# Storing some products of a gated feed-forward block as two split parts and loading the parts in place

## The chip, the cores and the metric

The kernel runs on one core of one Trainium2 chip. The metric is the time of one execution on the device in microseconds (us), lower is better. The engines are PE (TensorE), DVE (VectorE), ACT (ScalarE), POOL (GpSimd) and SP (SyncE, which here only issues DMAs). Each engine takes its instructions strictly in the order of its own list; an instruction that waits holds everything behind it on that engine.

## The reference

One layer works on x of 1024 tokens by 1024 channels in float32. The two feed-forward blocks (D_FF = 2816) are what the change touches:

```python
def swiglu(x, wg, wu, wd):
    return (jax.nn.silu(x @ wg) * (x @ wu)) @ wd

def reference(x, ...):
    x = x + 0.5 * swiglu(rmsnorm(x, norm_ffn1[l]), ffn1_wg[l], ffn1_wu[l], ffn1_wd[l])
    h = rmsnorm(x, norm_mix[l])
    ...  # one projection, an mLSTM group and an RG-LRU group, one output projection
    x = x + 0.5 * swiglu(rmsnorm(x, norm_ffn2[l]), ffn2_wg[l], ffn2_wu[l], ffn2_wd[l])
    return rmsnorm(x, norm_final)
```

## The kernel before

Activations lie with channels on the 128 partitions and tokens along the free axis, in two halves of 512 tokens. Every matmul is made three times, (high, high), (high, low) and (low, high): `split` (L107) writes a tile's high part with a CAST on ACT (L108) and its low part, the tile minus the high part, with a subtraction on DVE (L109).

`ffn` runs twice. Its inner product u = silu(gate) x up has 22 rows f of 128 channels. Rows 0 to 3 are made by `plain` (24 matmuls for each half and weight). Rows 4 to 21 are made in *units*: `Pair.run` (L543) multiplies a 2x2 block product with seven block products instead of eight. A unit has seven *steps* of 12 matmuls, s0 to s6, which use the factors B11, T1, T2, B21, T3, B22, T4 of the right-hand side in this order. s0, s2, s4 and s6 add up in one PSUM bank (X), s1 and s5 in another (Y), s3 has its own (Z). After each step `out(i, ...)` takes the running sum: out0, out1 and out2 are copies on ACT (`kept`, L613), out3 to out5 are additions on DVE (L617). So s2 must wait for out0, s4 for out2, s5 for out1 and s6 for out4, because each adds on to a bank that has to be read first.

The last product of the block, with wd, uses rows 0 to 15 of u in eight more units (`down`), in two groups of four. Their seven factors are sums and differences of u that `Sink` makes on POOL (`first_sum` L482: T1; `sums` L490 to L495: T2, T3, T4) when a pair of rows (f even, f odd) is there, and stores to DRAM (`f_d`, 1 MB each, `store` L463). Class `Stored` loads them back: `fetch(i)` brings factor i in plain float32 into a staging tile while the unit before is running, `split(i)` makes the two parts (L109 into `bop`) once that unit has finished step i. In the down units each `out` is a scaled copy on ACT (L646) that POOL adds to x with an accumulating DMA (L647). Rows 16 to 21 of u are stored whole (`u_d`), loaded by `act` and split, and go into an ordinary product at the end of the block (L325).

Temporary 128x512 tiles come from one pool of three buffers (`t2`, L100); rows f even of the first 16 lie in two tiles of their own (`even`). Odd rows, T4 and now and then a square use `t2`. Before the first block, `norm.square` takes the squares of x for the norm on ACT and adds them up on POOL (L184), tile by tile behind the loads.

The order on each engine is made by a scheduler when the program is built, from the written order and from costs of its own; it isn't what the chip finds ready at run time.

Of the kernel before, what the change touches and what calls it, by code (L numbers as in the profile page):

```python
# [8 lines left out]
F32 = mybir.dt.float32  # L9
R32 = mybir.dt.float32r  # L10
# [23 lines left out]
def hymba_block_kernel(ctx: ExitStack, tc, xT, chv, qkv, kblk, wgate, bgate, up1, db1, dn1, up2, db2,  # L34
# [13 lines left out]
    r_d = [dram.tile([P, T], F32, name=f"r_d{i}") for i in range(NK)]  # L48
    u_d = [dram.tile([P, T], F32, name=f"u_d{i}") for i in range(NF - 16)]
    f_d = [{n: dram.tile([P, 4, 512], F32, name=f"f_d{i}{n}")  # L50
            for n in ("B11", "T1", "T2", "B21", "T3", "B22", "T4")} for i in range(2)]
# [155 lines left out]
    class Norm:  # L207
# [22 lines left out]

        def square(self, xs, m, h, wait, first=1):
            add_square(self.pool, self.acc[h], row(xs, m)[:, half_of(h)], m)
            if m == NK - 1:
                def stats():
                    rs = row_rstd(self.pool, self.pool, self.acc[h][0], "n")
                    defer(wait, lambda: self.spread(xs, h, rs))
                defer(first, stats)
# [100 lines left out]
    def row(xs, t):  # L338
        return xs[t // 4][:, t % 4]
# [66 lines left out]
    class Stored:  # L406

        def __init__(self, bx, late, src):  # L410
            self.bx, self.late, self.src, self.ops, self.raw = bx, late, src, {}, {}

        def fetch(self, i):
            if i >= len(FACTORS):
                return
            src = self.src[FACTORS[i]].rearrange("p a n -> p (a n)")
            if i % 2 == 0:
                r = wup.tile([P, 2, T], R32, tag="wu", name="stage", bufs=4).bitcast(F32)
                nc.sync.dma_start(out=r.rearrange("p a n -> p (a n)"), in_=src)
                self.raw[i] = [r[:, 0], r[:, 1]]  # L420
            else:
                self.raw[i] = [raw_tile(), self.late.tile([P, T], F32, tag="rb_late", name="stage",
                                                          bufs=1)]
                for c, r in enumerate(self.raw[i]):
                    nc.sync.dma_start(out=r, in_=src[:, c * T:(c + 1) * T])

        def split(self, i):
            t = self.ops[FACTORS[i]] = factor_tile(self.bx, FACTORS[i])
            for c, r in enumerate(self.raw.pop(i)):
                split(t[:, 0, 2 * c:2 * c + 2], t[:, 1, 2 * c:2 * c + 2],  # L430
                      r.rearrange("p (a n) -> p a n", a=2))
# [18 lines left out]
    class Sink:  # L450
# [6 lines left out]
        def tile(self, f):  # L457
            if f < BLOCKED and f % 2 == 0:
                return self.pool.tile([P, 512], F32, tag="acc", name="even", bufs=2)
            return self.tmp()  # L460

        def store(self, f, name, t):
            nc.sync.dma_start(out=f_d[f // 8][name][:, f % 8 // 2], in_=t)  # L463

        def done(self, f, h, t):
            if f >= BLOCKED:
                nc.sync.dma_start(out=u_d[f - BLOCKED][:, half_of(h)], in_=t)
                return
            r = self.rows.setdefault(f, {})
            r[h] = t  # L470
            if f % 2 == 0:
                if h == 0:
                    self.store(f, "B11", t)
                if len(r) == 2:
                    self.pending.append(lambda: self.first_sum(f))
                return
            self.store(f, ("B21", "B22")[h], t)
            if len(r) == 2:
                self.flush()
                self.sums(f)  # L480

        def first_sum(self, f):  # L482
            u = self.rows[f]
            nc.gpsimd.tensor_tensor(out=u[0], in0=u[1], in1=u[0], op=ALU.subtract)
            self.store(f, "T1", u[0])

        def sums(self, f):
# [7 lines left out]
            sub(out=t, in0=v[0], in1=u[0], op=ALU.subtract)  # L495
            self.store(f, "T4", t)

        def flush(self):
# [74 lines left out]
    def ffn(xs, norm, up, blocked, dn, source, after_row, load_next=lambda: None, last_pieces=halves,  # L573
# [3 lines left out]
        with tc.tile_pool(name="bx", bufs=3, reuse_waits="tile") as bx:  # L577
            with tc.tile_pool(name="up", bufs=1, reuse_waits="tile") as pool:
# [73 lines left out]
                for g in range(BLOCKED // 8):  # L652
                    factors = Stored(bx, norm.pool, f_d[g])
                    work += [(Pair(pool, blocked[g, 2 * j], blocked[g, 2 * j + 1]), factors, down(j))
                             for j in range(4)]

                p = work[0][0]
                late = [plain(0, 0), plain(0, 1), plain(1, 0)]
                for f in late:
                    f()  # L660
                late = [plain(1, 1)]
                late.append(plain(0, 2))
                for f in late:
# [23 lines left out]
                def act(n):  # L687
                    t = half_tile(("a", n // 2), bx, "bx", n % 2)
                    acts[n] = t
                    split(t[:, 0], t[:, 1], load(u_d[n]))  # L690

# [56 lines left out]
    for h in range(2):  # L748
        for m in range(NK):
            nc.sync.dma_start(out=row(xs, m)[:, half_of(h)], in_=xT[m, :, half_of(h)])  # L750
            norm.scale(xs, m, h)
            norm.square(xs, m, h, 2, (2, 3)[h])
            if (h, m) in ((0, 0), (0, 1), (0, 5), (0, 7)):
                first.append((weights if first else weights_by_half)(up1[len(first)]))
    norm_mix = Norm(nrm, "nm")

# [747 lines left out]
```

## Time and profile before

| | |
|---|---|
| three runs | 2144.03, 2145.83, 2145.97 us; median 2145.83 |
| profiled execution | 2142.77 us, span of the trace 2141.1 us |
| PE busy | 2074.8 us (97%), 9526 matmuls |
| DVE, ACT, POOL busy | 1215.5 (57%), 921.9 (43%), 861.2 us (40%) |
| HBM read, written | 168.89 MB, 65.55 MB |

The profile lists when each instruction ran and what ended the idle time before it. The first feed-forward block takes the first 630 us or so of the span plus an ordinary product to about 700 us, the second the last 690 us. PE is nearly always busy, so what counts is where PE sits idle, and for what. PEclk is the clock granted to PE as a share of 2.4 GHz.

### The profile page before, as it was taken

The page shows a single profiled execution, that of the slowest core. Times are in us where ns is not written, and L with a number is a line of the kernel's source. Part 1 is how long each engine was busy: PE and PEld are TensorE (multiplying, and loading weights), DVE is VectorE, ACT ScalarE, POOL GpSimd, SP SyncE. Part 2 cuts the span into 40 slices and gives each one's busy share as a digit, 9 for nine tenths or more (in the row PEclk, how much of TensorE's full clock was granted, in tenths as well). Part 3 has the DMA queues.
Part 4 walks back from the last instruction along what each step waited for, and adds up shares of the span by engine and source line. Part 5 has one row for each costly group of instructions (what it writes and reads, how often), then busy time and mean ns, then how long its engine had stood idle before and what let it go on. Part 6 is the DMA issues. An engine that isn't in the chain of part 4 may idle for free.

```text
span 2141.1 us, 25174 instructions
## 1 busy us (share of the span) xinstructions
PE 2074.8 (97%) x9526; PEld 1708.2 (80%) x9526; DVE 1215.5 (57%) x1618; ACT 921.9 (43%) x1337; POOL 861.2 (40%) x614
## 2 busy tenths in 40 slices
PE   8999999999999999999999999999999999999998
PEld 6878888878778788878878888777888888877877
DVE  7954444473434455665538998878753444474334
ACT  5333333354542355555546554233333333365443
POOL 4465455445634212232311122433555555354623
PEclk9999999999999999999999999999999999999999
DMA  4143232278891311132246332121243323388852
GB/s 169 64 172 123 99 118 94 89 227 186 216 248 66 111 34 66 67 108 89 86 143 218 105 109 69 60 92 71 94 172 114 113 99 104 106 219 232 185 144 79
DMA packets 112194, 265.45 MB, mean 124 GB/s; under 512 B 10949, under 2 KB 29637, under 8 KB 109001
## 3 DMA queue, kind: packets, MB, share of 16 engines
q1 hardware_dynamic: 95944, 234.48, 32.4%
q0 software_dynamic: 16128, 29.37, 7.8%
q8 instruction: 74, 1.21, 0.2%
q14 instruction: 48, 0.39, 0.1%
HBM read 168.89 MB, written 65.55 MB: 110 GB/s over the span
## 4 chain that ended last, share of the span: by engine, by line
PE 75%; DVE 9%; DMA 4%; issue 4%; ACT 3%; POOL 3%; SPq 1%; POOLq 0%; ACTq 0%; DVEq 0%
PE bank_b L441 39%; PE bank_a L308 13%; PE bank_b L325 9%; PE bank_b L308 4%; PE bank_s L325 3%; PE bank_a L904 2%; DVE wu L109 1%; DVE bop L109 1%; PE bank_s L1181 1%; PE bank_b L1210 1%; DMA raw<-in_up_dram 1%; DMA raw<-in_dn_dram 1%; DVE xs L1335 1%; DMA stage<-f_d1B 1%; DVE w L1325 1%
## 5 line engine op out<-in xcount | busy, mean ns | idle before, releaser
L441 PE MATMUL bank_b<-bop,wu 128*128 128x512 f32 x3744 | 863.0, 390 | 14.5 <-ACT wu L108 5.5
L441 PEld LDWEIGHTS bank_b<-bop,wu 128*128 128x128 f32 x3744 | 702.7, 188 | 166.6 <-ACT ct L646 8.0
L109 DVE TENSOR_TENSOR wu<-raw,wu 128x1024 fp32r<-128x1024 f32 (+1 forms) x283 | 337.9, 1210 | 438.2 <-ACT wu L108 437.4
L108 ACT CAST wu<-raw 128x1024 fp32r<-128x1024 f32 (+1 forms) x283 | 245.3, 887 | 264.5 <-PE bank_b L441 146.2
L308 PE MATMUL bank_a<-hT,wu 128*128 128x512 f32 x1488 | 345.7, 391 | 3.1 <-ACT t L932 1.4
L308 PEld LDWEIGHTS bank_a<-hT,wu 128*128 128x128 f32 x1488 | 278.0, 188 | 63.9 <-POOL hT L109 1.9
L516 POOL TENSOR_TENSOR raw<-raw 128x512 f32<-128x512 f32 x52 | 74.0, 1423 | 312.1 <-DMA raw<-in_up_dram 274.5
L441 PE MATMUL bank_b<-bop,wd 128*128 128x512 f32 x624 | 159.9, 408 | 12.7 <-ACT ct L646 9.7
L308 PE MATMUL bank_b<-hT,wu 128*128 128x512 f32 x720 | 165.5, 390 | 1.0 <-DVE wu L109 1.0
L325 PE MATMUL bank_b<-u,wu 128*128 128x512 f32 (+1 forms) x768 | 162.2, 364 | 1.2 <-DVE xs L1335 0.8
L308 PEld LDWEIGHTS bank_b<-hT,wu 128*128 128x128 f32 x720 | 135.2, 188 | 29.5 <-DVE wu L109 1.4
L613 ACT COPY ct<-bank_b 128x512 f32<-128x512 f32 x108 | 63.1, 587 | 218.1 <-PE bank_b L441 202.7
L441 PEld LDWEIGHTS bank_b<-bop,wd 128*128 128x128 f32 x624 | 122.5, 198 | 42.8 <-ACT ct L646 13.4
L647 POOL DMA_DIRECT2D xs<-ct x112 | 100.3, 972 | 135.1 <-ACT ct L646 111.9
L325 PEld LDWEIGHTS bank_b<-u,wu 128*128 128x128 f32 x768 | 132.0, 189 | 25.6 <-DVE xs L1335 2.5
L617 DVE TENSOR_TENSOR ct<-ct,bank_b 128x512 f32<-128x512 f32 x108 | 73.8, 684 | 89.8 <-PE bank_b L441 89.8
L184 POOL TENSOR_TENSOR acc<-acc,t 128x512 f32<-128x512 f32 (+1 forms) x52 | 70.0, 1347 | 113.5 <-ACT t L182 112.2
L646 ACT ACTIVATE ct<-bank_b 128x512 f32<-128x512 f32 x112 | 65.6, 595 | 111.1 <-PE bank_b L441 59.4
L325 PE MATMUL bank_s<-wu 128*128 128x512 f32 x384 | 97.9, 396 | 1.7 <-ACT wu L108 1.0
L869 DVE SCALAR_TENSOR_TENSOR t<-bank_a,ch,t 128x1023 f32<-128x1023 f32 (+2 forms) x48 | 61.4, 1278 | 46.3 <-ACT t L866 45.8
L523 POOL TENSOR_TENSOR raw<-raw 128x512 f32<-128x512 f32 x52 | 81.7, 1570 | 9.3 <-DVE wu L109 9.3
L518 POOL TENSOR_TENSOR raw<-raw 128x512 f32<-128x512 f32 x52 | 83.2, 1601 | 0.0
(241 smaller groups left out, 2600.9 us busy)
## 6 DMA issues: line engine op xcount, KB each, us to landing
raw<-in_up_dram SPq DMA_DIRECT2D x87, 512.0 KB, 3.8
xs<-ct POOLq DMA_DIRECT2D x112, 256.0 KB, 5.5
raw<-in_db_dram SPq DMA_DIRECT2D x32, 512.0 KB, 4.4
raw<-in_win_dram SPq DMA_DIRECT2D x32, 512.0 KB, 3.5
xs<-in_xT_dram SPq DMA_DIRECT2D x32, 256.0 KB, 6.0
x_d<-xs SPq DMA_DIRECT2D x32, 256.0 KB, 2.0
v_d<-u SPq DMA_DIRECT2D x8, 1024.0 KB, 3.8
v<-v_d SPq DMA_DIRECT2D x16, 512.0 KB, 7.0
```

Source lines behind the costliest of these rows:

```text
L108: nc.scalar.copy(hi, src)
L109: (eng or nc.vector).tensor_tensor(out=lo, in0=src, in1=hi.bitcast(F32), op=ALU.subtract)
L184: eng.tensor_tensor(out=box[0], in0=box[0], in1=sq, op=ALU.add)
L308: nc.tensor.matmul(ps, lhsT=w[:, a, k * P:(k + 1) * P], rhs=hT[b][half][:, k], start=(k == 0 and n == 0), stop=(k == NK - 1 and n == 2))
L325: nc.tensor.matmul(ps, lhsT=w[:, a, m * P:(m + 1) * P], rhs=u[:, b, pieces[h]], start=(i == 0 and n == 0), stop=(i == len(lhs) - 1 and n = ...
L441: nc.tensor.matmul(ps, lhsT=w[:, a, k * P:(k + 1) * P], rhs=u[:, b, k], start=(first and k == 0 and n == 0), stop=(k == 3 and n == 2), ski ...
L516: add(out=self.s[:, lo], in0=self.u[:, lo], in1=self.u[:, hi], op=ALU.add)
L518: add(out=self.u[:, lo], in0=self.g[:, lo], in1=self.u[:, lo], op=ALU.subtract)
L523: nc.gpsimd.tensor_tensor(out=self.g[:, hi], in0=self.g[:, hi], in1=self.s[:, hi], op=ALU.subtract)
L617: nc.vector.tensor_tensor(out=t[a], in0=t[a], in1=ps, op=ALU.add)
L646: nc.scalar.activation(part, ps, AF.Identity, scale=0.5)
L647: nc.gpsimd.dma_start(out=xt, in_=part, accum_op=ALU.add)
```

## The change

Three of the seven stored factors (T1, B21, B22; `IN_PARTS`) are split when they are made, by the new `store_parts`, and stored as two parts, 2 MB instead of 1 MB each. In `store_parts` the high part is a new `t2` tile; the low part takes the place of the source, except for T1, which needs both (`keep`). When they are loaded, both parts go straight into the operand tile, with no staging and no CAST and subtraction, but only when that tile's buffer is free. B21 and B22 are now stored at the end of `sums`, behind T2, T3 and T4. Rows 16 to 21 of u are treated in the same way, and take `even` tiles. The squares of x before the first block are written behind all loads and added up on DVE, and the first eight `plain` products change their order a little. The accumulating DMAs of `down` remain.

```diff
+    IN_PARTS = ("T1", "B21", "B22")
+    f_d = [{n: dram.tile([P, 2, 4, 512] if n in IN_PARTS else [P, 4, 512], F32, name=f"f_d{i}{n}")
...
         def fetch(self, i):
-            if i >= len(FACTORS):
+            if i >= len(FACTORS) or FACTORS[i] in IN_PARTS:
                 return
...
         def split(self, i):
             t = self.ops[FACTORS[i]] = factor_tile(self.bx, FACTORS[i])
+            if FACTORS[i] in IN_PARTS:
+                for a in range(2):
+                    nc.sync.dma_start(out=t[:, a].bitcast(F32), in_=self.src[FACTORS[i]][:, a])
+                return
...
         def tile(self, f):
-            if f < BLOCKED and f % 2 == 0:
+            if f >= BLOCKED or f % 2 == 0:
                 return self.pool.tile([P, 512], F32, tag="acc", name="even", bufs=2)
+            self.flush()
             return self.tmp()
...
+        def store_parts(self, f, name, t, keep=False):
+
+            hi = t2(self.pool).bitcast(R32)
+            lo = (t2(self.pool) if keep else t).bitcast(R32)
+            split(hi, lo, t)
+            for a, part in enumerate((hi, lo)):
+                nc.sync.dma_start(out=f_d[f // 8][name][:, a, f % 8 // 2], in_=part.bitcast(F32))
...
             if f >= BLOCKED:
-                nc.sync.dma_start(out=u_d[f - BLOCKED][:, half_of(h)], in_=t)
+                hi, lo = t2(self.pool).bitcast(R32), t.bitcast(R32)
+                split(hi, lo, t)
+                for a, part in enumerate((hi, lo)):
+                    nc.sync.dma_start(out=u_d[f - BLOCKED][:, a, half_of(h)], in_=part.bitcast(F32))
...
-            self.store(f, ("B21", "B22")[h], t)
...
-            self.store(f, "T1", u[0])
+            self.store_parts(f, "T1", u[0], keep=True)
...
             sub(out=t, in0=v[0], in1=u[0], op=ALU.subtract)
             self.store(f, "T4", t)
+            self.store_parts(f, "B21", v[0])
+            self.store_parts(f, "B22", v[1])
...
-                    split(t[:, 0], t[:, 1], load(u_d[n]))
+                    nc.sync.dma_start(out=t.bitcast(F32), in_=u_d[n])
...
-            norm.square(xs, m, h, 2, (2, 3)[h])
...
+    for h in range(2):
+        for m in range(NK):
+            norm.square(xs, m, h, (1, 2)[h], (4, 5)[h], nc.vector)
```

ACT's list in the unit that follows row f = 15 (the same place stands behind each odd row from 5 to 15 of both blocks), before: the CAST of s6's weights (`wd`), out0, out1 and out2 (`ct` from `bank_b`), then weights for the next unit.

```order
L108 CAST wd_2463<-raw_2348 128x512
L613 COPY ct_2480<-bank_b_2466 128x512
L613 COPY ct_2498<-bank_b_2467 128x512
L613 COPY ct_2516<-bank_b_2466 128x512
L108 CAST wu_2550<-raw_2500 128x1024
```

The same place with the change; `t2_2546` and `t2_2547` are the two halves of row 15.

```order
L110 CAST wd_2567<-raw_2439 128x512
L626 COPY ct_2584<-bank_b_2570 128x512
L110 CAST t2_2557<-t2_2546 128x512
L626 COPY ct_2602<-bank_b_2571 128x512
L110 CAST t2_2562<-t2_2547 128x512
L626 COPY ct_2620<-bank_b_2570 128x512
L110 CAST wu_2654<-raw_2604 128x1024
```

Between out0 and out1 the high part of B21 is made, and between out1 and out2 the high part of B22. T4, the high part of B21 and the high part of B22 were given the same one of the three `t2` buffers, one after the other.

SP's list around the change from the first to the second group of down units in the first block, before (`f_d1...` are the factors of the second group, `raw` and `stage` tiles in which they wait to be split, `in_db1` weights):

```order
L419 DMA stage_3694<-f_d1B11_122 128x2048
L425 DMA raw_3748<-f_d1B21_125 128x1024
L419 DMA stage_3722<-f_d1T2_124 128x2048
L425 DMA stage_3749<-f_d1B21_125 128x1024
L419 DMA stage_3776<-f_d1T3_126 128x2048
L425 DMA raw_3802<-f_d1B22_127 128x1024
L419 DMA stage_3827<-f_d1T4_128 128x2048
L425 DMA stage_3803<-f_d1B22_127 128x1024
L118 DMA raw_3897<-in_db1_dram 128x1024
```

And with the change:

```order
L419 DMA stage_3828<-f_d1B11_122 128x2048
L120 DMA raw_4013<-in_db1_dram 128x1024
L427 DMA bop_3873<-f_d1T1_123 128x2048
L419 DMA stage_3852<-f_d1T2_124 128x2048
L427 DMA bop_3873<-f_d1T1_123 128x2048
L419 DMA stage_3900<-f_d1T3_126 128x2048
L427 DMA bop_3921<-f_d1B21_125 128x2048 x2
L419 DMA stage_3945<-f_d1T4_128 128x2048
L427 DMA bop_3965<-f_d1B22_127 128x2048 x2
L120 DMA raw_4015<-in_db1_dram 128x1024
```

T1 is no longer loaded ahead of this place, each of the three factors comes as two transfers of 1 MB into the operand tile, and a weight tile of the unit after next stands behind all of them.

## Rows read from the trace of the kernel before

**Rows 1.** Waits of PE: what it waited for: us in total, times, longest

```profile
PE bank_b L441 <- ACT ct L646: 14.3, 12, 3.2
...
PE bank_b L441 <- ACT wu L108: 5.5, 2, 2.8
```

**Rows 2.** Timeline of unit f = 12: start us, us, engine, line, operation, tiles

```profile
267.54 2.29 POOL L632 TENSOR_TENSOR t<-ct 128x512 f32<-128x512 f32 x1
267.73 16.48 PE L441 MATMUL bank_b<-bop,wu 128*128 128x512 f32 x72
...
269.91 1.62 POOL L490 TENSOR_TENSOR even<-t,even 128x512 f32<-128x512 f32 x1
270.64 0.59 ACT L613 COPY ct<-bank_b 128x512 f32<-128x512 f32 x1 [2.04 <-PE bank_b L441]
271.49 1.29 POOL L492 TENSOR_TENSOR even<-t,even 128x512 f32<-128x512 f32 x1
...
273.98 1.29 POOL L495 TENSOR_TENSOR t<-t,even 128x512 f32<-128x512 f32 x1
275.30 0.32 SPq L463 DMA_DIRECT2D f_d1T<-t  x1
...
276.14 0.59 ACT L613 COPY ct<-bank_b 128x512 f32<-128x512 f32 x1 [2.13 <-PE bank_b L441]
```

**Rows 3.** Stores of T factors, 200 to 330 us, then T4's alone (200 to 300 us)

```profile
DMA to landing us min/median/max: 2.3/2.7/4.0
...
f_d1T<-t SPq DMA_DIRECT2D x2, 256.0 KB, 3.1
```

**Rows 4.** PE's timeline: two stalls of about 3 us

```profile
128.84 5.49 PE L441 MATMUL bank_b<-bop,wd 128*128 128x512 f32 x12 [3.04 <-DVE ct L617]
...
624.46 3.03 PE L441 MATMUL bank_b<-bop,wd 128*128 128x512 f32 x12 [3.18 <-ACT ct L646]
```

**Rows 5.** Windows of 1 us there: length, PE busy, PEclk, DMA share, GB/s

```profile
127.00:128.00 1.00, 0.00 (x0) 0.97 0.82 272
...
134.00:135.00 1.00, 1.00 (x4) 0.62 1.04 408
...
625.00:626.00 1.00, 1.00 (x6) 1.00 1.11 283
```

**Rows 6.** Timeline: T4 of row 3 in the first block, then unit f = 4 of the second

```profile
125.62 0.32 SPq L463 DMA_DIRECT2D f_d0T<-t  x1
...
1546.63 16.48 PE L441 MATMUL bank_b<-bop,wu 128*128 128x512 f32 x72
...
1557.81 0.32 SPq L463 DMA_DIRECT2D f_d0T<-t  x1
```

**Rows 7.** DMA queues: packets, MB, share of 16 engines over the span

```profile
q1 hardware_dynamic: 95944, 234.48, 32.4%
```

**Rows 8.** Windows of 5 us: length, busy PE, PEld, DVE, ACT, POOL, PEclk, DMA share, GB/s

```profile
465.00:470.00 5.00, 4.40 (x20) 3.32 (x19) 5.00 (x5) 3.10 (x5) 3.20 (x4) 1.00 0.74 231
...
540.00:545.00 5.00, 3.98 (x10) 2.87 (x11) 4.25 (x4) 4.00 (x6) 2.17 (x2) 0.60 1.07 325
...
620.00:625.00 5.00, 1.82 (x8) 1.22 (x7) 3.08 (x3) 3.21 (x5) 1.07 (x2) 1.00 1.05 353
```

**Rows 9.** Timeline of the start of the span

```profile
5.25 0.75 DVE L113 SCALAR_TENSOR_TENSOR hT<-xs,ch,hT 128x512 fp32r<-128x512 f32 x1 [4.33 <-ACT hT L112]
...
11.41 5.85 DVE L113 SCALAR_TENSOR_TENSOR hT<-xs,ch,hT 128x512 fp32r<-128x512 f32 x4
...
21.23 4.33 PE L301 MATMUL bank_b<-hT,wu 128*128 128x512 f32 x11 [2.26 <-DVE hT L113]
...
25.35 5.74 PE L308 MATMUL bank_b<-hT,wu 128*128 128x512 f32 x24
```

**Rows 10.** Window of 30 us in the plain rows of the first block

```profile
60.00:90.00 30.00, 28.98 (x129) 23.67 (x128) 28.82 (x27) 7.45 (x9) 14.78 (x8) 1.00 0.24 87
```

More of the change, by code (lines that the diff above doesn't have):

```diff
@@ L48, in hymba_block_kernel @@
     r_d = [dram.tile([P, T], F32, name=f"r_d{i}") for i in range(NK)]
-    u_d = [dram.tile([P, T], F32, name=f"u_d{i}") for i in range(NF - 16)]
-    f_d = [{n: dram.tile([P, 4, 512], F32, name=f"f_d{i}{n}")
+    u_d = [dram.tile([P, 2, T], F32, name=f"u_d{i}") for i in range(NF - 16)]
+    IN_PARTS = ("T1", "B21", "B22")
+    f_d = [{n: dram.tile([P, 2, 4, 512] if n in IN_PARTS else [P, 4, 512], F32, name=f"f_d{i}{n}")
             for n in ("B11", "T1", "T2", "B21", "T3", "B22", "T4")} for i in range(2)]
@@ L229, in scale, with square @@
                          chan(self.gain, m))
-        def square(self, xs, m, h, wait, first=1):
-            add_square(self.pool, self.acc[h], row(xs, m)[:, half_of(h)], m)
+        def square(self, xs, m, h, wait, first=1, eng=None):
+            add_square(self.pool, self.acc[h], row(xs, m)[:, half_of(h)], m, eng)
             if m == NK - 1:
@@ L406, in hymba_block_kernel, with __init__ @@
     class Stored:
-        def __init__(self, bx, late, src):
-            self.bx, self.late, self.src, self.ops, self.raw = bx, late, src, {}, {}
+        def __init__(self, bx, src):
+            self.bx, self.src, self.ops, self.raw = bx, src, {}, {}
         def fetch(self, i):
-            if i >= len(FACTORS):
+            if i >= len(FACTORS) or FACTORS[i] in IN_PARTS:
                 return
[L416 to L425, printed above, removed]
+            r = wup.tile([P, 2, T], R32, tag="wu", name="stage", bufs=4).bitcast(F32)
+            nc.sync.dma_start(out=r.rearrange("p a n -> p (a n)"),
+                              in_=self.src[FACTORS[i]].rearrange("p a n -> p (a n)"))
+            self.raw[i] = [r[:, 0], r[:, 1]]
         def split(self, i):
             t = self.ops[FACTORS[i]] = factor_tile(self.bx, FACTORS[i])
+            if FACTORS[i] in IN_PARTS:
+                for a in range(2):
+                    nc.sync.dma_start(out=t[:, a].bitcast(F32), in_=self.src[FACTORS[i]][:, a])
+                return
             for c, r in enumerate(self.raw.pop(i)):
@@ L652, in ffn @@
                 for g in range(BLOCKED // 8):
-                    factors = Stored(bx, norm.pool, f_d[g])
+                    factors = Stored(bx, f_d[g])
                     work += [(Pair(pool, blocked[g, 2 * j], blocked[g, 2 * j + 1]), factors, down(j))
@@ L658, in ffn @@
                 late = [plain(0, 0), plain(0, 1), plain(1, 0)]
+                late.pop(0)()
+                late.append(plain(1, 1))
                 for f in late:
                     f()
-                late = [plain(1, 1)]
-                late.append(plain(0, 2))
+                late = [plain(0, 2)]
                 for f in late:
```

## Prediction

> **What bounds the kernel now.** I read the table of busy times first: PE works 97% of the span, so a gain can come only from its few idle places, and any wait that is added to PE is lost in full. Then the list of PE's waits: in the feed-forward blocks the largest entry is 14.3 us for ACT's copies in the down units, next to it 5.5 us for ACT's weight splits [rows 1]; ACT is late there because it stands in its list at a CAST whose staging tile is still being loaded. In the middle of the block, units f = 5 to 21, the list has no wait of PE at all. The timeline of such a unit shows why: call S = 267.73 the start of s0; six steps take 16.48 us, 2.75 each, and out2 is copied at S + 8.41, before s4 wants to start at S + 10.99 [rows 2]. So 2.6 us of slack stand between ACT and PE. The timeline of the DMAs then shows when the sums of a pair of rows get out: POOL makes row f's half, T2, T3 and T4 one after the other, and T4's store is issued at S + 7.57 [rows 2].
>
> **The change, part by part.**
>
> *Splitting B21 and B22 when they are made.* The work itself, two CASTs and two subtractions of 128x512 for each odd row, would lie beside PE: both engines have idle time in these units. What matters is where the CASTs stand and for what they wait. The lists show B21's between out0 and out1, and B22's between out1 and out2, behind each of the six odd rows 5 to 15 of either block. B21's high part takes T4's buffer, so ACT waits until T4's store has landed; B22's high part takes the same buffer again, so ACT waits until B21's store has landed. Behind it in ACT's list stands out2, and for out2 waits s4 on PE. Worked out on the unit above: T4's store is issued at S + 7.57 and lands 3.1 us later [rows 2, 3], S + 10.67. The CAST is as large as one of the copies, 0.59 us [rows 2]: S + 11.26. Its store lands after the median 2.7 us [rows 3]: S + 13.96. The second CAST: S + 14.55. out2: S + 15.14. s4 wanted S + 10.99: PE stands still for 4.15 us, where it didn't wait. The order in which POOL makes T4 is the same as before, and POOL isn't freed sooner by anything here. Twelve such units: 50 us. With the shortest landing, 2.3 us twice, a stall is 2.95 us (35 us in all), with the longest, 4.0 us twice, 6.35 us (76 us) [rows 3]. out1, held until S + 11.9, is wanted by s5 only, after s4. T1's split stands between out0 and out1 of the odd unit, and there is no second link in its chain: nothing for it.
>
> *The clock behind such a stall.* The trace shows what a stall does afterwards. PE stood from 125.80 to 128.84 [rows 4]; the granted clock fell to half at 127.94 and came back at 134.76 [rows 5], that is from 2.1 to 9.0 us behind the start of the stall. Not each stall does it: after the one of 3.18 us that ended at 624.46 the clock stayed full [rows 4, 5]. Of the five longest stalls in the feed-forward blocks that I looked at (2.3 to 3.2 us) four were followed by half clock. A stall of 4.15 us leaves 4.8 us of work at 1.2 GHz, 2.4 us lost. Twelve times 0.8 times 2.4: 23 us. Bounds: none at all, and 12 x 3.4 = 41 us.
> The Trainium skill (TensorE: Matmul & The Clock Gate, Part 1) says that half clock is the state that PE returns to whenever it has been idle for long enough, and that activity alone releases it. By that rule a stall as long as these would always be followed by it, and the sum would be 29 us in place of 23; the stall that ended at 624.46 went the other way, so I keep the count of the rows.
>
> *The first unit, f = 4.* Here B21 and B22 of row 3 stand before and shortly after out2. In the second block T4's store is issued 11.18 us after the unit's start [rows 6]; with 3.1 us, a CAST and out2 that makes S + 15.46, a stall of 4.5 us, and 0.8 x 2.3 us for the clock: 6.3 us. In the first block T4's store goes out at 125.62 [rows 6]; out2 is done at 129.90, s4 and s5 take 5.5 us, and s6 begins at 135.4, where it began at 128.84 [rows 4]: 6.6 us. Together 13 us, between 0 (if the plain rows end sooner) and 20 (the subtraction for B22 stands ahead of out3 in DVE's list).
>
> *Squares late.* At the start DVE made four scaled tiles in 5.85 us, 1.46 each, while POOL added squares, and 0.75 alone; PE waited 2.26 us for the last, and the first 48 matmuls were over at 25.35 [rows 9]. Without the squares in between some 7 us can go there. But what follows is set by DVE: it is busy 28.82 of 30 us [rows 10] up to the first unit, the row statistics now come later in PE's list, and DVE gets six subtractions more there (rows 0 to 3), at 0.75 us 4.5 us. I take 0, between -7 and +4.5.
>
> *Loading the parts.* Before, a down group loads seven factors of 1 MB; now three of them are 2 MB, 3.15 MB more. SP's queue moved 234.48 MB in 32.4% of the span [rows 7], 2.96 us for a MB with all 16 engines at work, so each group costs 9.3 us more of DMA time, and so does the end of the block (six rows of u, 0.52 MB more each). What of it PE sees depends on how full the DMAs are there: into the first group the share is 0.74, between the groups 1.07, at the end 1.05 [rows 8]. T1 is no longer loaded ahead, and the unit after next has a weight behind all of it on SP. In return ACT and DVE don't stand at those loads any more, which takes away some of the waits of rows 1. I take 3 us for the first group, 8 for the second, 5 for the end: 16 us a block, 32 in all. Bounds: -20 (all of the 14.3 + 5.5 us of rows 1 go and the bytes are hidden) and +56 (six times 9.3).
> The Trainium skill (DMA: Bandwidth & Descriptors, Anatomy of one DMA) gives 436 GB/s beside a fixed part. At that rate 3.15 MB take 7.2 us, and the 32 us would be 25, by an estimate from that page. The row gives 338 GB/s for this kernel's own transfers, and I stay with it.
>
> *The rows 16 to 21 of u.* Their two CASTs stand before out0, and wait for halves that are there by S + 2.1; the pool's other buffers are free by then. Nothing.
>
> *Sum.* 50 + 23 + 13 + 0 + 32 = 118 us. Against the profiled execution, 2142.77 us, that is 2260.8; it lies 3.1 us under the median of the runs shown, so 2264 us.
>
> **The rivals.**
> *The chain stays hidden, and the kernel gets faster.* If the two stores and CASTs are over before s4 needs out2, PE sees nothing of them, and what is left is relief: up to 19.8 us from rows 1 and 7 at the start, 2145.8 - 26.8 = 2119 us. The point from which it decides is S + 10.4 for the end of B22's CAST, 4.15 us sooner than worked out: both stores would have to land in under 1 us, and the shortest of the trace is 2.3 [rows 3]. For it speaks only that the scheduler put the CASTs there as if they were ready.
> *The loads pay for themselves.* The stalls of the chain come, but ACT and DVE, no longer held by staging tiles, take away more than the bytes add: -20 in place of +32, 2212 us. For it: rows 1 name ACT and not a DMA; against it: DMA share 1.07 [rows 8].
> *The bytes come through whole.* +56 in place of +32, and half clock behind each of the six places, 6 x 2.4 = 14 us: 2302 us. For it: the weights behind the factors; against it: the first group's share of 0.74.
> *Full clock after the stalls.* 23 and 3 us less: 2238 us, inside the forecast's own range.
>
> **How the numbers follow.** Forecast 0.60 (full clock included), with a range of its own from 2225 to 2300; loads pay for themselves 0.18; bytes come through whole 0.14; chain hidden 0.06; the parts cancel 0.02. The low end must take in the second with short landings: 2145.8 + 35 + 13 - 20 + some clock, about 2190. The high end takes in the third with stalls of 5 us (10 us more) and a little: 2320. Faster by over 0.2% has the 0.06, the same within 0.2% (what a measurement of this kernel can't tell from no change) 0.02, slower the rest, 0.92.
>
> **What would show it.** In the list of PE's waits a new entry at L441 for the copy `ct` of `kept`, about twelve times some 4 us, each in a unit with an even f; in the timeline of such a unit a CAST `t<-t` on ACT that waited for a store, and out2 behind it near S + 15; half clock behind most of them. In the down groups DMA shares of 1 for longer, and PE waiting for loads rather than for ACT. I am wrong if out2 stands near S + 8.4 in those units: then the buffers, or the stores' landing, are not what I read from the lists.

## The result, and the profile after

The changed kernel takes 2258.27 us (median of four runs, 2252.49 to 2262.91), the kernel before 2145.90 beside it: a ratio of 1.0524, 95% interval 1.0499 to 1.055. It is slower, by about what was forecast (2264 us). The profiled execution took 2257.13 us, 114.4 more than that of before; its span is 2255.4 us, PE is busy for 94% of it, and the mean granted clock fell from 0.991 to 0.968.

PE's list of waits comes first (what it waited for: us in total, times, longest).

```profile
PE bank_b L441 <- ACT ct L626: 62.1, 15, 7.0
PE bank_b L441 <- ACT wu L110: 18.1, 6, 3.9
PE bank_b L327 <- ACT wu L110: 13.3, 2, 8.6
...
PE bank_b L441 <- ACT ct L659: 2.8, 5, 0.9
```

L626 is `kept`: the copies out0 to out2. Before had one such wait, of 2.0 us; now there are 15, 12 in the middle of the blocks and 3 in the two units f = 4. L659 is the old L646, whose 14.3 us [rows 1] have nearly gone; at L327, the last product of a block, two waits for weights have come.

The timeline of unit f = 12 (start, us, engine, line, operation, tiles; in brackets the idle time before and what ended it) answers to [rows 2]. S is now 294.32.

```profile
294.32 11.04 PE L441 MATMUL bank_b<-bop,wu 128*128 128x512 f32 x48
...
300.51 1.28 POOL L506 TENSOR_TENSOR t<-t,even 128x512 f32<-128x512 f32 x1
301.83 0.32 SPq L464 DMA_DIRECT2D f_d1T<-t  x1
...
305.04 0.62 ACT L110 CAST t<-t 128x512 fp32r<-128x512 f32 x1 [7.21 <-DMA f_d1T<-t]
305.57 0.58 ACT L626 COPY ct<-bank_b 128x512 f32<-128x512 f32 x1
305.69 3.79 SPq L472 DMA_DIRECT2D f_d1B<-t  x4
...
307.79 0.62 ACT L110 CAST t<-t 128x512 fp32r<-128x512 f32 x1 [1.65 <-DMA f_d1B<-t]
308.31 0.58 ACT L626 COPY ct<-bank_b 128x512 f32<-128x512 f32 x1
...
308.94 5.75 PE L441 MATMUL bank_b<-bop,wu 128*128 128x512 f32 x24 [3.58 <-ACT ct L626]
```

Read down it is the chain of the forecast: T4's store goes out at S + 7.51, ACT's CAST for B21 waits 7.21 us for its landing, the CAST for B22 waits for the landing of B21's store, out2 is copied at S + 14.0, and s4 starts at S + 14.6 in place of S + 11. T4's store landed 3.2 us after its issue, B21's 2.1. The landing of the stores of T factors from 200 to 330 us (min, median, max) answers to [rows 3]; most of them are now T1's parts, which landed in 2.0 us, while T2, T3 and T4 took 2.3 to 3.9:

```profile
DMA to landing us min/median/max: 2.0/2.0/3.9
```

Behind this stall the clock stayed full. Two units later it did not (windows of 1 us: busy PE, PEld, DVE, ACT, POOL, PEclk, DMA share, GB/s); here PE stood from 347.3 to 350.94:

```profile
349.00:350.00 1.00, 0.00 (x0) 0.00 (x0) 0.00 (x0) 0.22 (x1) 0.00 (x0) 1.00 0.88 340
...
352.00:353.00 1.00, 1.00 (x4) 0.81 (x3) 1.00 (x1) 0.87 (x2) 0.00 (x0) 0.50 0.66 256
...
355.00:356.00 1.00, 1.00 (x6) 0.83 (x5) 0.42 (x1) 0.00 (x0) 0.00 (x0) 1.00 0.80 324
```

The 24 matmuls of s4 and s5 take 5.75 us at full clock and 7.3 us there. Ten of the twelve stalls were followed by half clock.

The end of the first block, in the timeline of SP, ACT and PE: six loads of u, one weight asked for behind them, and its landing 23 us later.

```profile
656.49 6.27 SPq L704 DMA_DIRECT2D u<-u_d  x6
...
664.80 0.33 SPq L120 DMA_DIRECT2D raw<-in_dn_dram  x1
...
687.94 1.04 ACT L110 CAST wu<-raw 128x1024 fp32r<-128x1024 f32 x1 [10.21 <-DMA raw<-in_dn_dram]
689.04 3.36 PE L327 MATMUL bank_b<-u,wu 128*128 128x512 f32 x7 [8.61 <-ACT wu L110]
```

SP's queue moved 37.76 MB more than before [rows 7] (packets, MB, share of 16 engines):

```profile
q1 hardware_dynamic: 106312, 272.24, 34.3%
```

Each term of the sum has a measured counterpart, from the starts of units in the two timelines (time of after minus time of before, or the excess of a unit over 19.04 us):

| term | forecast, us | measured, us |
|---|---|---|
| stall ahead of s4, 12 units | 50 | 48.2 (block 1: 23.0, block 2: 25.2) |
| half clock behind them | 23 | 23.7 (8.9 and 14.8) |
| first unit, f = 4 | 6.6 + 6.3 | 8.2 + 4.1 |
| squares late | 0 | 4 gained by the end of the first 48 matmuls (the next start at 21.18, before at 25.35 [rows 9]), given back by f = 5; inside the 8.2 |
| loads: first group, between groups, end, both blocks | 6 + 16 + 10 = 32 | 7.5 + 9.9 + 13.7 = 31.1 |
| mixer between the blocks | none | -0.6 |
| sum | 118 | 114.7 of 114.4 |

### The profile page after: what moved, and what is told of

Its sections match the earlier page's. It is cut to its first block, busy times and chain, and to the rows that moved or that the text cites. A ratio compares the mean times of both kernels' runs of the same rounds, so it can differ in the third digit from the quotient of the medians.

```text
span 2255.4 us, 25335 instructions
## 1 busy us (share of the span) xinstructions
PE 2115.9 (94%) x9526; PEld 1734.8 (77%) x9526; DVE 1214.2 (54%) x1666; ACT 928.6 (41%) x1373; POOL 842.0 (37%) x602
## 3 DMA queue, kind: packets, MB, share of 16 engines
q1 hardware_dynamic: 106312, 272.24, 34.3%
## 4 chain that ended last, share of the span: by engine, by line
PE 62%; DMA 10%; DVE 10%; POOL 9%; issue 5%; ACT 4%; SPq 0%; POOLq 0%; ACTq 0%; DVEq 0%
PE bank_b L441 27%; PE bank_a L310 13%; PE bank_b L327 8%; PE bank_b L310 4%; PE bank_s L327 3%; DMA raw<-in_dn_dram 2%; DMA raw<-in_up_dram 2%; DVE wu L111 2%; PE bank_a L920 2%; DVE bop L111 1%; POOL raw L531 1%; PE bank_b L303 1%; PE bank_s L1197 1%; DMA f_d1T<-t 1%; ACT wu L110 1%
## 5 line engine op out<-in xcount | busy, mean ns | idle before, releaser
L441 PE MATMUL bank_b<-bop,wu 128*128 128x512 f32 x3744 | 904.3, 402 | 86.9 <-ACT ct L626 62.1
L441 PEld LDWEIGHTS bank_b<-bop,wu 128*128 128x128 f32 x3744 | 726.8, 195 | 255.6 <-ACT ct L626 69.0
L111 DVE TENSOR_TENSOR wu<-raw,wu 128x1024 fp32r<-128x1024 f32 (+1 forms) x283 | 325.3, 1168 | 326.5 <-ACT wu L110 325.5
L529 POOL TENSOR_TENSOR raw<-raw 128x512 f32<-128x512 f32 x52 | 71.6, 1377 | 394.1 <-DMA raw<-in_up_dram 317.6
L327 PE MATMUL bank_b<-u,wu 128*128 128x512 f32 (+1 forms) x768 | 167.3, 371 | 16.7 <-ACT wu L110 13.3
L327 PEld LDWEIGHTS bank_b<-u,wu 128*128 128x128 f32 x768 | 134.8, 193 | 42.8 <-ACT wu L110 14.1
L441 PE MATMUL bank_b<-bop,wd 128*128 128x512 f32 x624 | 153.9, 396 | 1.2 <-ACT ct L659 0.9
L659 ACT ACTIVATE ct<-bank_b 128x512 f32<-128x512 f32 x112 | 66.5, 598 | 157.8 <-PE bank_b L441 84.7
L626 ACT COPY ct<-bank_b 128x512 f32<-128x512 f32 x108 | 62.9, 585 | 110.0 <-PE bank_b L441 110.0
L111 DVE TENSOR_TENSOR t<-t,t 128x512 fp32r<-128x512 f32 x32 | 23.2, 726 | 154.1 <-ACT t L110 154.1
L327 PE MATMUL bank_s<-wu 128*128 128x512 f32 x384 | 97.9, 396 | 2.2 <-ACT wu L110 1.5
L536 POOL TENSOR_TENSOR raw<-raw 128x512 f32<-128x512 f32 x52 | 82.7, 1590 | 39.7 <-DVE wu L111 39.7
L186 POOL TENSOR_TENSOR acc<-acc,t 128x512 f32<-128x512 f32 (+1 forms) x40 | 50.0, 1251 | 111.3 <-ACT t L184 110.6
L885 DVE SCALAR_TENSOR_TENSOR t<-bank_a,ch,t 128x1023 f32<-128x1023 f32 (+2 forms) x48 | 61.4, 1278 | 46.2 <-ACT t L882 45.7
## 6 DMA issues: line engine op xcount, KB each, us to landing
u<-u_d SPq DMA_DIRECT2D x12, 1024.0 KB, 14.6
```

What stands on the lines that cost most here:

```text
L111: (eng or nc.vector).tensor_tensor(out=lo, in0=src, in1=hi.bitcast(F32), op=ALU.subtract)
L327: nc.tensor.matmul(ps, lhsT=w[:, a, m * P:(m + 1) * P], rhs=u[:, b, pieces[h]], start=(i == 0 and n == 0), stop=(i == len(lhs) - 1 and n = ...
L441: nc.tensor.matmul(ps, lhsT=w[:, a, k * P:(k + 1) * P], rhs=u[:, b, k], start=(first and k == 0 and n == 0), stop=(k == 3 and n == 2), ski ...
L529: add(out=self.s[:, lo], in0=self.u[:, lo], in1=self.u[:, hi], op=ALU.add)
L536: nc.gpsimd.tensor_tensor(out=self.g[:, hi], in0=self.g[:, hi], in1=self.s[:, hi], op=ALU.subtract)
L626: nc.scalar.copy(c, ps)
```

## The experiments

All times are medians, ratios are to runs of the kernel before on the same chip.

| kernel | us | ratio, 95% interval |
|---|---|---|
| T4 in place | 2183.27 | 1.017 (1.015 to 1.019) |
| three factors only | 2233.53 | 1.0401 (1.0379 to 1.0424) |
| squares only | 2144.92 | 0.9991 (0.998 to 1.0002) |
| six rows of u only | 2162.24 | 1.0074 (1.0052 to 1.0097) |
| T4 in place, u whole | 2164.27 | 1.0083 (1.0068 to 1.0098) |
| T1 only | 2161.02 | 1.0062 (1.0048 to 1.0077) |
| last three rows of u only | 2161.85 | 1.0073 (1.0061 to 1.0085) |
| last two rows of u only | 2158.31 | 1.0058 (1.0046 to 1.007) |
| the same, loaded behind the weights | 2152.26 | 1.0027 (1.0017 to 1.0038) |
| that order alone | 2145.71 | 1.0002 (0.9993 to 1.0011) |
| T1 only, loads on POOL's queue | 2176.96 | 1.0145 (1.0132 to 1.0159) |
| B22 only | 2175.15 | 1.0143 (1.0127 to 1.0158) |

To see where each kernel loses, its timeline of PE is laid beside that of before: start of step s6 (the matmuls `bank_b<-bop,wd`) of the same unit, minus its start in before, us. The profiled execution of T1 alone was the fastest of its runs (2154.78 us), so its column shows some 6 us less than its median; that of before was 3 us under its median.

| s6 of | after | T4 in place | factors | u six | T1 | B22 | u two | u two, behind |
|---|---|---|---|---|---|---|---|---|
| f = 5, block 1 | 7.9 | 5.6 | 4.7 | -0.4 | 5.6 | 6.9 | -1.6 | -0.3 |
| f = 20 | 40.1 | 7.6 | 37.8 | -0.4 | 5.6 | 8.2 | -1.6 | -0.3 |
| third down unit | 43.7 | 10.4 | 38.5 | 3.1 | 3.5 | 10.0 | 1.5 | 3.4 |
| seventh down unit | 48.8 | 16.5 | 42.8 | 2.9 | 8.4 | 14.1 | 1.3 | 3.8 |
| last down unit | 45.7 | 13.4 | 43.3 | -0.5 | 8.2 | 14.0 | -2.0 | 4.0 |
| f = 4, block 2 | 59.1 | 27.2 | 53.6 | 8.8 | 8.2 | 23.3 | 6.7 | 3.4 |

**Is it the one buffer?** T4 is written over T2's tile, so that the high part of B21 finds a free `t2` buffer. Stores, CASTs, subtractions, loads and bytes (272.24 MB on SP's queue) stay. The scheduler moved the two CASTs one place up in ACT's list: B21's now stands ahead of out0, B22's ahead of out1.

```diff
-            t = t2(self.pool)
-            sub(out=t, in0=v[0], in1=u[0], op=ALU.subtract)
-            self.store(f, "T4", t)
+            sub(out=u[0], in0=v[0], in1=u[0], op=ALU.subtract)
+            self.store(f, "T4", u[0])
```

> The kernel after, with one edit: T4 is subtracted in place, into the tile that held T2, so it takes no t2 buffer and the CAST for the high part of B21 gets one that is free. All the stores, CASTs, subtractions and loads of the change stay. Theory (the chain of one buffer through two store landings holds ACT, and PE waits for out2): B21's CAST no longer waits for T4's store; only B22's still waits for a store (2.0 us in the profile of after), so out2 should stand near S + 9.7 to S + 10.3, ahead of S + 10.88 where s4 wants it. Of the 62.1 us that PE waits for ct at L626 less than 10 stay, the half clock behind them (23.7 us) goes, and the time falls by 65 to 80 us, to 2178 to 2193 us. Rival (the extra CASTs, subtractions and store bytes beside the units cost the time themselves, whichever buffer they use): within 15 us of 2258.

It took 75 us fewer than after, as the theory had it. PE's waits for the copies, and the timeline of unit f = 14 (S = 313.35; T4 is the subtraction at 319.58):

```profile
PE bank_b L441 <- ACT ct L625: 16.5, 5, 8.3
```

```profile
313.35 16.48 PE L441 MATMUL bank_b<-bop,wu 128*128 128x512 f32 x72
...
314.81 0.62 ACT L110 CAST t<-t 128x512 fp32r<-128x512 f32 x1 [0.58 <-DVE t L645]
...
319.58 1.29 POOL L505 TENSOR_TENSOR even<-t,even 128x512 f32<-128x512 f32 x1
320.90 0.32 SPq L464 DMA_DIRECT2D f_d1T<-even  x1
320.91 0.69 DVE L111 TENSOR_TENSOR t<-t,t 128x512 fp32r<-128x512 f32 x1 [5.01 <-POOL even L505]
...
321.65 0.62 ACT L110 CAST t<-t 128x512 fp32r<-128x512 f32 x1 [4.79 <-DVE t L111]
322.17 1.07 ACT L625 COPY ct<-bank_b 128x512 f32<-128x512 f32 x2
```

B21's CAST comes at S + 1.5, B22's at S + 8.3, out2 is done by S + 9.9, an us ahead of s4, and six steps run through in 16.48 us. Where the twelve units lost 48.2 us by stalls and 23.7 by half clock, 2.0 us are left (two waits, 0.5 and 0.9 us). Three waits in the units f = 4 make the other 15.1 us of the row, so more stayed than the 10 us expected; these two units still lose 5.9 and 4.9 us. In the twelve units the splits and their stores cost PE nothing by themselves; the buffer did. The rival falls. The new place in the list is not what helped: B22's CAST now holds back out1 as well as out2.

**The parts one by one.** Factors alone (after, with u whole and the squares early), squares alone and u alone (before, with that part):

> The kernel after without two of its parts: rows 16 to 21 of u are stored whole again, and the squares of x are early on POOL as before; only T1, B21 and B22 are in parts. Theory: the stalls and the half clock of the twelve units (72 us), those of the two units f = 4 (12 us) and the loads into and between the groups (about 4 and 5 us for each block, less the 3 us of a stall that went) stay, the end of the block (7 to 10 us for each block) goes: 2258 less 14 to 20, 2238 to 2244 us. Rival (the end of the block costs nothing by itself, its wait is the rest of an earlier delay of the queues): 2252 to 2262 us.

> The kernel before with one part of the change: the squares of x are written behind all loads and added up on DVE, and the first plain products come in the new order. Theory (4 us are gained at the first 48 matmuls and lost again, since DVE sets the pace up to the first unit and has six subtractions more): within 4 us of before, 2142 to 2150 us. Rival (the 4 us at the start stay gained when no parts stand behind them): 2140 to 2142 us, PE's first unit some 4 us sooner than before.

> The kernel before with one part of the change: rows 16 to 21 of u are split when made and stored as two parts, and loaded straight to their place. Theory: nothing in the units, since their CASTs wait for buffers that are free, and 5 to 10 us at the end of each block, where six loads of 1 MB take the place of six of 0.5 MB and PE waits for them: before plus 10 to 20 us, 2156 to 2166 us. Rival (the 3 us stall ahead of the last down unit goes because ACT no longer waits with those splits, and the bytes are hidden): 2138 to 2143 us.

The factors alone came out 24.7 us under after, 5 more than the theory's end. By the two profiled executions, 23.7 us apart, 12.4 of it lie at the ends of the blocks, behind the seventh down unit, a little less than the theory had. It didn't have another 10.3 us: from f = 20 to the seventh down unit, after loses 8.7 us in each block, the factors alone 5.1 and 2.1. Of these, 8.9 lie ahead of the third down unit, where the rows of u alone lose 3.5 and 4.7 us; so they are probably u's, but no run shows it.

The squares alone are no change. They gain at the start, where the first 48 matmuls are over at 20.42 and not at 25.35. Most of it goes at one wait for DVE, 4.6 us at 77.33 (the second line), where before waited 1.0 (the last line, of before), and s6 of f = 4 starts at 128.77, where before had 128.84 [rows 4]:

```profile
20.42 16.48 PE L308 MATMUL bank_b<-hT,wu 128*128 128x512 f32 x72
...
77.33 29.95 PE L308 MATMUL bank_b<-hT,wu 128*128 128x512 f32 x118 [4.59 <-DVE wu L109]
...
128.77 5.49 PE L441 MATMUL bank_b<-bop,wd 128*128 128x512 f32 x12 [3.24 <-DVE ct L617]
```

```profile
74.21 32.48 PE L308 MATMUL bank_b<-hT,wu 128*128 128x512 f32 x142 [1.02 <-DVE wu L109]
```

The rows of u alone cost 15.8 us, in the theory's range, but not all at the end of a block: nothing in the units, 3.5 us up to the third down unit (4.7 in block 2), 3 us back at the last, 9 to the next block. The first of these, which the theory didn't have, is a stall of 3.8 us ahead of s6 in the first down unit (before: 0.7), with half clock behind it. All four kernels with rows of u in parts and the factors whole have it, 3.7 to 3.8 us in each block. The three parts alone add up to 101 us (87.1 - 1.5 + 15.8), together they cost 112; as runs of one kernel lie 8 to 10 us apart here (after 2252 to 2263, the factors alone 2228 to 2236), nothing is read from the difference.

**T4 in place, with u whole**, the two edits together:

> T4 in place, as in the run before that did only this (2183.3 us), and rows 16 to 21 of u stored whole again. What is left of the change are the three factors in parts and the late squares. Theory (the end of a block pays for the 3.15 MB more that its loads of u bring): the two waits of 8.7 us ahead of the last product, 15.4 us together, go, and the 3 us stall of before in the last down unit comes back: 2183 less 10 to 24 us, 2159 to 2173 us. The upper part of that loss is what the kernel with the factors alone showed against after (25 us), the lower what u alone showed against before (16 us) less the stall. Rival (the waits at the end are the rest of the queue of factor loads): 2178 to 2186 us.

It took 19 us fewer, inside the theory's range, and the stall of the last down unit came back (3.9 us there). The parts that are kept still don't beat before: 17 us are left.

**Which factor, and do the bytes count?** One factor in parts, and the rest as in the kernel before (shown against after):

```diff
-    IN_PARTS = ("T1", "B21", "B22")
+    IN_PARTS = ("T1",)
```

```diff
-    IN_PARTS = ("T1", "B21", "B22")
+    IN_PARTS = ("B22",)
```

> The kernel before with T1 alone stored and loaded in parts; B21 and B22 are stored and loaded whole as before, u too, squares as before. Theory (a factor costs by the buffer its split waits for, and by its bytes): T1 has no second link in its chain, so no stall at L441 for ct in the middle of the blocks; 1 MB more for each group of down units, a third of what the three factors bring, costs 0 to 3 us a block: before plus 0 to 6 us, 2146 to 2152 us. Rival (every split that is made beside the units costs PE time, about 6 us for the two of B21 and B22, so 2 to 3 us a unit pair for T1): before plus 24 to 36 us, 2170 to 2182 us.

> The kernel before with B22 alone in parts: the same bytes as with T1 alone, another factor. By the lists the high part takes the buffer of B21 and not that of T4, so it waits for no store behind T4's subtraction: out2 near S + 9.5, no stall at s4 in the middle units (by the theory of the one buffer; by its rival, that each split beside a unit costs PE time, 2 to 3 us for each of 12). For the loads: if T1's lost head start is what costs 5 us a block between the groups, they fall to 0 to 2 us here, before plus 0 to 6 us, 2146 to 2153 us; if any factor in place costs that, 2154 to 2162 us.

Both keep f = 6 to 20 all but free of stalls (the table's second line, less its first: 0.0 and 1.3 us), in agreement with the theory of the one buffer. With B22 alone the CAST waits for B21's store and not T4's:

```profile
244.08 0.32 SPq L470 DMA_DIRECT2D f_d1T<-t  x1
244.86 0.62 ACT L110 CAST t<-t 128x512 fp32r<-128x512 f32 x1 [4.83 <-DMA f_d1B<-t]
245.39 1.07 ACT L630 COPY ct<-bank_b 128x512 f32<-128x512 f32 x2
```

But both expectations on the time were missed, T1's by 9 us, B22's by 13. The first reason is the first unit. There, in B22's kernel, the CAST stands in ACT's list ahead of out0 and out1, and its buffer, B21's tile, is free only when POOL has subtracted T4:

```profile
124.68 0.62 ACT L110 CAST t<-t 128x512 fp32r<-128x512 f32 x1 [9.92 <-POOL t L511]
125.21 1.07 ACT L630 COPY ct<-bank_b 128x512 f32<-128x512 f32 x2
...
125.84 12.47 PE L447 MATMUL bank_b<-bop,wu 128*128 128x512 f32 x46 [12.53 <-ACT ct L630]
```

Before stands still for 5.0 us in this unit (2.0 and 3.0), so 7.5 us are new; in block 2 the stall is 7.0 us, where before had none. In the kernel with T1 alone its CAST waits for POOL ahead of two copies in unit f = 5, a stall of 4.88 us. The second reason is between the groups (third to seventh down unit of block 1): 4.9 us with T1, 4.1 with B22, where all three cost 5.0 in after, 4.3 alone and 6.1 with T4 in place. A third of the bytes costs nearly the same, with either factor, so neither the bytes nor T1's lost head start explains it alone. In the list of B22's kernel ACT waits there for POOL, which makes the weight sums late:

```profile
571.70 1.05 ACT L110 CAST wu<-raw 128x1024 fp32r<-128x1024 f32 x1 [3.23 <-POOL raw L534]
...
576.33 4.61 PE L447 MATMUL bank_b<-bop,wd 128*128 128x512 f32 x12 [4.04 <-ACT ct L663]
```

**Is it SP's order there?** T1's loads are moved to POOL's queue:

```diff
-                    nc.sync.dma_start(out=t[:, a].bitcast(F32), in_=self.src[FACTORS[i]][:, a])
+                    nc.gpsimd.dma_start(out=t[:, a].bitcast(F32), in_=self.src[FACTORS[i]][:, a])
```

> The kernel with T1 alone in parts (2161.0 us), with its two loads for each group issued by POOL and not by SP. The bytes and the wait for the operand tile stay. Theory (between the groups PE pays because SP, standing at a load that waits for its operand tile, holds back the plain factors and weights behind it): the 4.6 to 5 us a block between the groups fall to 0 to 2 us, 2150 to 2155 us. Rival (the DMA engines are full there and 1 MB more is paid for wherever it is issued): 2158 to 2164 us. If POOL's own accumulating transfers are held behind the two loads, it is slower than that.

It came out 16 us slower than T1 on SP, and PE's waits for ct at L661 rise from 14.0 to 33.3 us. That looks like the outcome that the last sentence names, but the trace shows another reason. The longest waits stand behind ACT's CASTs of plain factors, which SP loads:

```profile
551.94 1.99 ACT L110 CAST bop<-stage 128x1024 fp32r<-128x1024 f32 x2 [6.14 <-DMA stage<-f_d1T]
...
556.86 5.49 PE L447 MATMUL bank_b<-bop,wd 128*128 128x512 f32 x12 [6.03 <-ACT ct L661]
```

No copy of L661 waited for an accumulating transfer (11.1 us with T1 on SP), and these transfers landed after a median of 5.4 us (6.2 with T1 on SP). The loss lies in the first group, 10 and 9 us more than with T1 on SP; between the groups it stays, 4.4 and 4.9 us, against the theory. But with the edit the scheduler also changed the order on ACT, so the run changes more than the queue and does not tell the theory from its rival.

**The end of a block: bytes or order?** Only the last three, or two, of the six rows of u in parts (`> 2` and `> 3`):

```diff
+                if not f - BLOCKED > 3:
+                    nc.sync.dma_start(out=u_d[f - BLOCKED][:, half_of(h)], in_=t)
+                    return
                 hi, lo = t2(self.pool).bitcast(R32), t.bitcast(R32)
...
-                    nc.sync.dma_start(out=t.bitcast(F32), in_=u_d[n])
+                    if n > 3:
+                        nc.sync.dma_start(out=t.bitcast(F32), in_=u_d[n])
+                    else:
+                        split(t[:, 0], t[:, 1], load(u_d[n]))
```

> The kernel before with the last three of the six rows 16 to 21 of u in parts; the first three stay whole and are split when loaded. Theory (at the end of a block PE pays for the bytes that its loads bring over what fits): half the extra bytes, 1.57 MB, 4.7 us by the row of the queue, so the wait of 8.5 us ahead of the last product falls to 3 to 5 us a block, and with the 3 us stall of the last down unit gone the time is before plus 0 to 4 us, 2146 to 2150 us. Rival (the wait is there because one weight tile stands behind the loads of u in SP's list, whatever their bytes): in this kernel four weight tiles and not one stand behind them, the wait stays at 8 us or grows, 2158 to 2170 us.

> The kernel before with the last two of the six rows 16 to 21 of u in parts. Theory (bytes over what fits): 1.05 MB more, 3.1 us, so the wait ahead of the last product is 0 to 3 us a block; the stall of the last down unit goes in part: before less 4 to before plus 2 us, 2142 to 2148 us. Rival (place in SP's list, not bytes): as with three rows, 2158 to 2170 us.

The theory of bytes falls, and both times lie in the rival's range. In block 1, PE's wait ahead of the last product was 8.47 us with six rows, 7.70 with three and 7.83 with two; in block 2 it was 7.9, 8.3 and 7.0, waits for a copy of the last down unit included. The timeline of the kernel with two:

```profile
614.47 1.22 SPq L697 DMA_DIRECT2D u<-u_d  x2
615.79 4.63 SPq L118 DMA_DIRECT2D raw<-in_dn_dram  x3
...
630.84 1.04 ACT L108 CAST u<-raw 128x1024 fp32r<-128x1024 f32 x1 [7.55 <-DMA raw<-in_dn_dram]
...
634.51 4.85 PE L325 MATMUL bank_b<-u,wu 128*128 128x512 f32 x13 [7.83 <-ACT wu L108]
```

Then the same bytes with the two loads asked for behind the weights:

```diff
-                ends = ([(weight_row, 0), (act, 0), (act, 1)], [(act, 2), (act, 3)],
-                        [(act, 4), (act, 5), (weight_row, 1)], [(weight_row, 4), (weight_row, 5)],
-                        [(weight_row, 2)], [(weight_row, 3)], [])
+                ends = ([(weight_row, 0), (act, 0), (act, 1)], [(act, 2), (act, 3), (weight_row, 1)],
+                        [(weight_row, 4), (weight_row, 5)], [(weight_row, 2)],
+                        [(weight_row, 3)], [(act, 4), (act, 5)], [])
```

> The kernel with the last two rows of u in parts (2158.3 us), with one edit: at the end of a block the loads of these two rows are asked for behind the five weight tiles and not ahead of three of them. The bytes are the same and the buffer of the operand is the same. Theory (loads that may only start when the operand tile is free start late, and what stands behind them on SP lands late): the weights now land in time, and the two rows of u, wanted last, stand alone at the end of the queue; the wait of 7.8 us a block ahead of the last product falls to 0 to 2 us, and the time to before minus 4 to before plus 2 us, 2142 to 2148 us. Rival (the bytes and the late start alone, whatever the order): 2155 to 2160 us.

> The kernel before with nothing but that order at the end of a block (weights ahead of the last two rows of u); all rows of u whole, no part of the change. It is what the run beside it is to be read against. Both theories: no DMA is held there for an operand tile, so the order matters little: within 4 us of before, 2143 to 2151 us.

The first line is of the first down unit, the others are of the end of the block:

```profile
480.60 5.49 PE L441 MATMUL bank_b<-bop,wd 128*128 128x512 f32 x12 [3.79 <-ACT ct L652]
...
614.36 8.27 SPq L118 DMA_DIRECT2D raw<-in_dn_dram  x5
...
622.69 0.95 SPq L697 DMA_DIRECT2D u<-u_d  x2
...
628.46 4.61 PE L441 MATMUL bank_b<-bop,wd 128*128 128x512 f32 x12 [3.40 <-ACT ct L652]
632.91 2.88 PE L325 MATMUL bank_b<-u,wu 128*128 128x512 f32 x12
```

PE's wait for weights at the last product is gone, and the last down unit to block 2 costs -0.6 us in place of 8.7 (the table's last two columns); counted from the seventh unit, which leaves out the stall that comes and goes, -0.4 in place of 5.4. The time fell by 6 us only, and stayed 4 us above the range expected: ACT's CASTs stand ahead of the last outs again, and a stall in the last down unit, here 3.4 us, is back, as in before [rows 4]. What is left above before, 7 us, was lost earlier: 3.6 us in each block by the stall in the first down unit. That order without parts changes nothing.

## Why the prediction was right, step by step

**The chain of the two stores** is shown, by its rows in the profile of after and by the edit that gives T4 no buffer of its own and so takes it away. The stall was 4.0 us on average where 4.15 was worked out. That it came so close is in part luck: T4's store landed in 3.1 to 3.3 us against 3.1, but went out at S + 7.4 to 8.6, not always at 7.57; B21's store landed in 2.0 to 2.1 us, not in the 2.7 of [rows 3], and was mis-sized by 0.6 us. The DMA engines were less busy while B21's store was under way (shares 0.18, 0.47 and 0.89 from 305 to 308) than while T4's was (1.01 and 0.95 from 303 to 305; two of these windows, columns as above); that this is why it landed sooner isn't shown:

```profile
303.00:304.00 1.00, 1.00 (x6) 0.84 (x5) 0.00 (x0) 0.00 (x0) 0.00 (x0) 1.00 1.01 264
...
306.00:307.00 1.00, 0.00 (x0) 0.00 (x0) 0.39 (x1) 0.14 (x1) 0.00 (x0) 1.00 0.47 184
```

**The clock.** 23.7 us against 23. That half clock follows most but not all of such stalls is what [rows 5] had; ten of twelve here. The rule of the Trainium skill that was weighed there (TensorE: Matmul & The Clock Gate, Part 1) would have had twelve; two of the twelve went the other way, so the count of the rows, 0.8, was the better guide.

**The first unit** was right in sum, 12.3 against 13, by two errors of about 2 us. In block 2 the stall ahead of s4 was 3.3 us, not 4.5, and full clock followed. In block 1 there were two: 5.6 us behind T4's store, as worked out, and 7.0 us further up, which I didn't have: out0 and out1 stood behind T1's CAST, which waited for POOL, and behind operand splits that waited for DVE. T1 alone has 2.6 us at that place, the three factors with early squares 2.6, and the squares alone 1.6; the three kernels with late squares and the factors in parts have 6.9 to 8.3, so it takes both. The gain of the late squares paid for part of it (s0 starts 1.1 us sooner than before).

**T1 and rows 16 to 21: "nothing".** Right for the middle units, where the offset stays the same from f = 6 to 20 (T1 alone, u alone). Wrong at f = 5, where T1's CAST holds two copies for 4.9 us, and up to the third down unit, where the rows of u cost 3.5 and 4.7 us of their own.

**Squares late** came out as zero for the reason given, that DVE sets the pace: alone they give back at a wait of 4.6 us for DVE most of what they gain at the start, without the six subtractions that the forecast added.

**The loads** were right in size, 31 against 32, by luck, and wrong in their reason: into the first groups they cost 7.5 us against 6, between the groups 9.9 against 16, at the ends 13.7 against 10. I priced them by bytes and DMA share. The runs show that at the end of a block the price is one of order: the parts may only be asked for when the operand tile is free (with six rows of u the first at 610.57, the last at 616.37, where the plain rows were asked for at 597.03 and 611.72), and the weights queued behind them land too late; with the weights ahead the same bytes of two rows cost next to nothing there. Between the groups one factor costs nearly what three do; whether that is order too stays open, as the run on POOL's queue changed more than the queue. The relief in rows 1 was real (14.3 us to 2.8), and for it a wait for weights came in nearly every place.

## What to carry to other kernels

An instruction that needs a temporary buffer waits for whatever used that buffer last, and all that stands behind it on its engine waits too: before adding a split next to a copy that PE needs, follow the buffer back through every store that must land, and if one output can be written over an input that is done, do that. Loading straight to the operand saves casts but gives up the staging tile's head start; so ask first for what PE wants first, and put loads that must wait for a tile last in the queue.

## What the runs showed that was not expected

- From 200 to 330 us the stores of parts, 256 KB each, landed in 2.0 to 2.2 us, T1's as well, for which PE did not wait. The stores of T2, T3 and T4 in the same stretch, as large, took 2.3 to 3.9 us.
- T1's two loads for each group, moved from SP's to POOL's queue, cost 16 us (2176.96 against 2161.02), by waits behind CASTs of plain factors, and not for POOL's accumulating transfers.
- One CAST in front of two copies held PE for 12.5 us in a single unit (B22 alone, f = 4 of block 1), 7.5 us more than before lost there.
